# Retention queries and keys as a seven-product unit, T4 of the projections summed by DMA, and the norm2 transposes inside w_o

## The chip, the cores and the metric

The kernel runs on one core of one Trainium2 chip. The metric is the device time of one execution in microseconds, median of three runs. In the text TensorE is PE (its weight loads PEld), VectorE is DVE, ScalarE is ACT, GpSimd is POOL and SyncE is SP. DMAs are issued from SP's queue, and those that add to what lies in SBUF from POOL's.

## The reference, cut to what matters

One decoder block on x of 512 tokens by 1024 features, all in float32:

```python
h = rmsnorm(x, norm1_w)
rq, rk, rv, rg, mq, mk, mv, ga, gb = split(h @ w_in)   # 512, 512, 1024, 1024, 512, 512, 512, 1024, 1024 columns
rq = rotary(rq); rk = rotary(rk) * 128**-0.5            # 4 heads of 128
a = (silu(rg) * groupnorm(retention(rq, rk, rv))) @ w_ret_out
b = moba_attention(rmsnorm(mq), rmsnorm(mk), mv) @ w_moba_out   # 8 heads of 64, causal
x = x + (sigmoid(ga) * a + sigmoid(gb) * b) @ w_o
h2 = rmsnorm(x, norm2_w)
x = x + (silu(h2 @ w_ffn_gate) * (h2 @ w_ffn_up)) @ w_ffn_down  # hidden size 2816

def rotary(x):           # per head; halves of the 128 features
    return concat([x1 * cos - x2 * sin, x2 * cos + x1 * sin])
```

## The kernel before

**Products.** Every float32 operand is split in a high part of reduced precision and a rest, and a product of two tiles is three matmuls (high by high, high by rest, rest by high). A matrix product is cut in quarters, two by two. A plain quarter product takes eight block products. Most products use the Winograd variant of Strassen's method instead, with seven, named B11, T1, T2, B21, B22, T3 and T4 after the weight quarter or the sum of weight quarters that each uses; `wino_unit` issues them in the order of a string such as `NORMAL = "B11 T1 *1 T2 B21 B22 T3 / T4"`. What stands behind the slash, T4, is put off: it is issued at the `*1` of the next unit. Seven products of 24 matmuls of 256 columns make a unit, 168 matmuls.

**Weights.** A tile `raw` of 128 by 1024 comes by DMA. Its high part `wh` is a cast on ACT, its rest `wl` is a subtraction on DVE, and PE reads both. The sums T1 and T3 of two quarters come ready from the DMA: SP loads one quarter and POOL's DMA adds the other. T2 is T1 plus B22, and T4 is T2 plus B21, each an addition on DVE over 1024 columns (`make_sum`). In some units of the feed-forward part T4 is made by a third DMA on POOL instead, once T2 has been split (`t4dma`, `was_split`).

**Stages.** First come the queries and keys of MoBA, 47 us in (weights moving, plain product). Then follow projection units of 512 columns by a table, `ORDER`: rg 0, rk 0, rv 0, gb 0, rk 1, rv 1, rg 1, gb 1, then the output products b, ga, a. All are seven-product units except rk 0 and rk 1 (retention queries and keys of two heads each) and the output products a and b, which are plain: `feat_blocks` takes 32 weight tiles one by one, and each meets both token halves, six matmuls of 256 columns, 192 in a unit. Then w_o (`ALONE` order, 512 columns wide, 24 matmuls a product), the norm2 transposes, and the feed-forward part in four chunks, of which the last ends in an `ALONE` unit as well.

**Order.** Each engine runs its instructions in the order in which the code issues them. `advance` is called after each group of matmuls: it steps the weight pieces, with at most `AHEAD = (3, 4)` split pieces ahead of PE, and fires what `later(n, ...)` put off by n steps. `run_bg(1)` takes one step of background work (attention, retention scores and values, gates): after every 12 matmuls in a seven-product unit, after every 24 in a plain one.

**Around the change.** `rot_out` applies the rotary form to a finished group. In `wino_unit` the first product of a unit is copied into the bank Z by ACT (`p1`), and B21 accumulates on it. In `ALONE` units the last product, T4w, goes to banks W of its own, and DVE adds the shared part from X to the output tile beforehand (`u3`). `h2_turn(0)` transposes the upper token half after w_o's last product, with PE, four times four 128-column transposes; ACT makes the high parts `h` from them, DVE the rests, and the first feed-forward unit (`plain_unit`) needs both.

Of the kernel before, what the change touches and what calls it, by code (L numbers as in the profile page):

```python
# [42 lines left out]
ORDER = (("rg", 0), ("rk", 0), ("rv", 0), ("gb", 0), ("rk", 1), ("rv", 1), ("rg", 1), ("gb", 1), ("b", 0), ("b", 1), ("ga", 0), ("a", 0), ("ga", 1), ("a", 1))  # L43
WRQ = (0, 0)
RLAG = (1, 2, 3)
# [32 lines left out]
DOWN = "B11 B21 T1 T2 B22 T3 / T4"  # L78
ALONE = "B11 B21 T1 T2 B22 T3 T4w"


def weight_plan():
# [31 lines left out]
    for name, i in ORDER:  # L114
        if name == "rg":
            cols(C_RG + 512 * i)
        elif name == "rv":
            cols(C_RV + 512 * i)
        elif name == "rk" and WRQ[i]:
            wino("w_in", C_RQ + 256 * i, "w_in", C_RK + 256 * i)  # L120
        elif name == "rk":
            feat(sum([group("w_in", c + (2 * i + h) * P, KT) for h in (0, 1) for c in (C_RQ, C_RK)], []))
        elif name == "a":
            feat(sum([group("w_ret_out", (4 * i + ct) * P, KT) for ct in range(4)], []))
        elif name == "b":
# [41 lines left out]
def hybrid_block(ctx: ExitStack, tc: tile.TileContext, wall, xin, xtok, n2, cin, out):  # L167
# [108 lines left out]
    for u, unit in enumerate(plan):  # L276
        chunk_of[u] = chunk
        if unit[0] in "WX":
            ws = quarter_parts(unit)
            order = unit[2].split()  # L280
            if len(ws) > 1 or unit[2] == DOWN:
                t4dma.add(u)
# [13 lines left out]
            for q in order:  # L296
                if q == "/":
                    rest = True
                elif q[0] == "*":
                    for _ in range(int(q[1:])):  # L300
                        porder += left.pop(0) if left else []
                else:
                    x = [(u, (q[:3].rstrip("w"), j)) for j in range(len(ws))]
# [13 lines left out]
    assert not left  # L317
    wstate = {"next": 0, "live": 0, "cap": AHEAD, "load": 0, "drop": 0}
    wwait = []
# [400 lines left out]
    def feat_blocks(blocks, nbg=1):  # L720
# [3 lines left out]
        for b in blocks:  # L724
# [7 lines left out]
            mv = moving()  # L732
            if isinstance(mv, list):
                for i, m in enumerate(mv):
                    mm3(banks[g][:, i * 256:(i + 1) * 256], blk(u, pos % 16), m, first and i == 0, last, True)
            else:
                mm3(banks[g], blk(u, pos % 16), mv, first, last)
            pos += 1
# [52 lines left out]
    def wino_unit(w, ev, hooks={}):  # L791
# [13 lines left out]
        def third(*x):  # L805
            ev.c22(*x)
            if "T4w" in order:
                ev.u3(*x)

        def first(*x):  # L810
            ev.p1(*([*x, bank("Z")] if seed else x))

        whole = "T4w" in order
        seed = not wide and order[1] != "B21"
# [332 lines left out]
    def rot_out(h0):  # L1147
        def f(r, c, x):

            a, b = halves(nm("rot"))  # L1150
            hf = RDK // 2
            if h0 is None:
                c, h = c
                V.tensor_tensor(a, x, cosT, ALU.mult)
                V.tensor_tensor(b[:hf], x[hf:], sinT[hf:], ALU.mult)
                V.tensor_tensor(b[hf:], x[:hf], sinT[:hf], ALU.mult)
                V.tensor_tensor(a, a, b, ALU.add)
                (rqT, rkT)[c][h] = split(f"r{c}_{h}", a, None, SLAG[1])
                return
# [151 lines left out]

    def hmov(k):
        m = ("A11", "A21") if k < 4 else ("A12", "A22")
        return [hW(x, k % 4) for x in m]

    def rk_unit(n):
        h = 2 * n
        if WRQ[n]:
            wino_unit(hW, Quarters(rot_out(h)))
        else:  # L1320
            blocks = [((c, x), lambda k=k: hmov(k), k == 0, k == KT - 1,
                       lambda ps, c=c, x=x: later(1, lambda: rot_out(None)(0, (c, x), ps)))
                      for x in (h, h + 1) for c in (0, 1) for k in range(KT)]
            feat_blocks(blocks[:KT] + [wino_finish] + blocks[KT:])

# [102 lines left out]
    class Residual:  # L1428
# [29 lines left out]

        def u3(self, x, i):
            self.add(1, 0, x, i, ALU.add)  # L1460

        def c21w(self, w, i):
            self.add(1, 0, w, i, ALU.add, True)

        c21 = c21w

# [41 lines left out]
    def h2_turn(r):  # L1508

        pss, lows = [], []  # L1510
# [6 lines left out]
        for j in range(4):  # L1517
# [143 lines left out]
    for c in range(len(CHUNKS)):  # L1661
# [23 lines left out]
def _consts():  # L1685
# [60 lines left out]
```

## Time and profile before

| what | value |
|---|---|
| time, median of 3 runs | 794.83 us (792.03 to 795.05) |
| the profiled execution's own time | 794.83 us |
| its span, first to last instruction | 792.8 us |
| PE busy | 783.8 us, 99% |
| DVE busy | 648.2 us, 82% |
| ACT busy | 441.5 us, 56% |
| POOL busy | 64.9 us, 8% |
| DMA traffic | 126.47 MB, mean 160 GB/s |

The span is one execution. Outside it lie 2.0 us of that execution's time. A row's mean duration is from an instruction's start to its end; matmuls overlap, so that what a matmul costs PE is the distance from one start to the next. The busy share of PE counts a matmul's whole duration and says little on the rate; the idle time before an instruction, and what ended it, says where PE waited.

### The profile page before, as it was taken

How to read it: one execution, taken by the hardware profiler on the slowest of the kernel's cores; microseconds unless marked ns; L12 is line 12 of the kernel's file. 1: busy time of each engine (PE TensorE's matmuls, PEld its weight loads, DVE VectorE, ACT ScalarE, POOL GpSimd, SP SyncE). 2: the span in 40 equal slices, each digit the busy share in tenths (PEclk: the TensorE clock that was granted, in tenths of full speed). 3: DMA queues.
4: the chain of work that ended last, by engine and by line, in shares of the span. 5: the costliest groups of instructions: out<-in, count | busy, mean ns of one | idle time of the engine just before them, and what ended most of it. 6: DMA issues, size and time to landing. Idle time of an engine off the chain costs nothing.

```text
span 792.8 us, 13679 instructions
## 1 busy us (share of the span) xinstructions
PE 783.8 (99%) x5410; PEld 722.4 (91%) x5410; DVE 648.2 (82%) x978; ACT 441.5 (56%) x722; POOL 64.9 (8%) x85
## 2 busy tenths in 40 slices
PE   9999999999999999999999899999999999999998
PEld 6889998889999998998988799988999899988996
DVE  7889877977788678867679979889887988879787
ACT  8556764757437458643445566535554455644551
POOL 0004000000000000000001000011101110111000
PEclk9999999999999999999999999999999999999999
DMA  9843451524526546372899903589846893679602
GB/s 324 247 118 69 133 120 42 132 64 146 138 74 166 134 148 145 112 182 76 243 335 242 247 1 81 148 212 279 225 107 172 212 309 101 165 196 289 139 1 106
DMA packets 38223, 126.47 MB, mean 160 GB/s; under 512 B 4240, under 2 KB 4496, under 8 KB 38160
## 3 DMA queue, kind: packets, MB, share of 16 engines
q1 hardware_dynamic: 28224, 92.83, 33.8%
q0 software_dynamic: 9360, 31.72, 23.1%
q10 hardware_dynamic: 576, 1.05, 0.4%
q8 instruction: 42, 0.69, 0.4%
q14 instruction: 21, 0.17, 0.1%
HBM read 123.49 MB, written 2.10 MB: 158 GB/s over the span
## 4 chain that ended last, share of the span: by engine, by line
PE 91%; DVE 5%; DMA 2%; ACT 1%; issue 1%; SPq 0%; ACTq 0%
PE pm L219 82%; PE ps L219 8%; DMA raw<-wall 2%; DVE wl L219 1%; DVE h L219 1%; DMA xv<-xin 1%; DVE ws L219 1%; DVE xr L219 0%; DVE raw L219 0%; ACT sqh L911 0%; ACT wh L408 0%; ACT h L1503 0%; DVE xn L219 0%; DVE fb L219 0%; DVE gs L219 0%
## 5 line engine op out<-in xcount | busy, mean ns | idle before, releaser
L219 DVE TENSOR_TENSOR wl<-raw,wh 128x1024 fp32r<-128x1024 f32 x203 | 245.8, 1221 | 39.1 <-ACT wh L408 32.9
L408 ACT CAST wh<-raw 128x1024 fp32r<-128x1024 f32 (+1 forms) x224 | 219.3, 1006 | 62.4 <-DVE raw L219 38.3
L219 PE MATMUL pm<-h,wh 128*128 128x256 f32 x1248 | 226.9, 284 | 2.8 <-DVE h L219 1.5
L219 PEld LDWEIGHTS pm<-h,wh 128*128 128x128 f32 x1248 | 196.3, 193 | 3.9 <-DVE h L219 1.7
L219 PE MATMUL pm<-h,wl 128*128 128x256 f32 x624 | 177.2, 284 | 0.0
L219 PEld LDWEIGHTS pm<-h,wl 128*128 128x128 f32 x624 | 120.5, 193 | 0.0
L335 POOL DMA_DIRECT2D raw<-wall x56 | 49.3, 881 | 596.7 <-DMA raw<-wall 289.1
L219 PE MATMUL pm<-hA,wh 128*128 128x256 f32 x448 | 83.1, 285 | 0.0
L219 PEld LDWEIGHTS pm<-hA,wh 128*128 128x128 f32 x448 | 70.2, 191 | 1.1 <-issue 0.5
L219 PE MATMUL pm<-wh,hA 128*128 128x256 f32 (+1 forms) x304 | 69.3, 310 | 0.0
L219 PE MATMUL pm<-hA,wl 128*128 128x256 f32 x224 | 63.4, 283 | 0.0
L219 PE MATMUL pm<-wh,hS 128*128 128x256 f32 x320 | 62.8, 287 | 0.4 <-ACT pm L867 0.4
L219 DVE TENSOR_TENSOR raw<-raw,raw 128x1024 f32<-128x1024 f32 (+1 forms) x47 | 55.7, 1188 | 0.8
L219 PEld LDWEIGHTS pm<-wh,hA 128*128 128x128 f32 x304 | 51.1, 191 | 2.5
L219 PEld LDWEIGHTS pm<-wh,hS 128*128 128x128 f32 x320 | 51.6, 191 | 0.8 <-ACT pm L867 0.6
L219 DVE TENSOR_TENSOR xr<-xr,pm 128x512 f32<-128x512 f32 x74 | 48.2, 682 | 1.2 <-PE pm L219 1.0
L219 PE MATMUL pm<-hS,wh 128*128 128x256 f32 x256 | 47.3, 285 | 0.0
L219 PE MATMUL pm<-wl,hA 128*128 128x256 f32 (+1 forms) x152 | 46.5, 306 | 0.0
L219 PE MATMUL pm<-wl,hS 128*128 128x256 f32 x160 | 45.3, 283 | 0.3 <-DVE wl L219 0.3
L219 PEld LDWEIGHTS pm<-hA,wl 128*128 128x128 f32 x224 | 42.8, 191 | 0.0
L219 PEld LDWEIGHTS pm<-hS,wh 128*128 128x128 f32 x256 | 40.0, 192 | 0.1
L219 PE MATMUL pm<-wh,gsh 128*128 128x512 f32 x112 | 39.9, 391 | 0.0
(266 smaller groups left out, 1399.9 us busy)
## 6 DMA issues: line engine op xcount, KB each, us to landing
raw<-wall SPq DMA_DIRECT2D x153, 512.0 KB, 4.8
raw<-wall POOLq DMA_DIRECT2D x56, 512.0 KB, 7.2
raw<-wall SPq DMA_DIRECT2D x19, 256.0 KB, 4.0
raw<-wall POOLq DMA_DIRECT2D x9, 256.0 KB, 6.6
xr<-xtok SPq DMA_DIRECT2D x4, 512.0 KB, 7.2
out<-xr SPq DMA_DIRECT2D x8, 256.0 KB, 2.2
x<-xin SPq DMA_DIRECT2D x7, 256.0 KB, 4.8
raw<-wall ACTq DMA_DIRECT2D x4, 256.0 KB, 6.2
```

Source lines behind the costliest of these rows:

```text
L219: return f(out, *args, **kw)
L335: nc.gpsimd.dma_start(t[:, s], wall[c, :, s], accum_op=ALU.add)
L408: A.copy(h, src)
```

## The change

- Both rk units become seven-product units (`WRQ` and the plain branch are gone). `rot_out` works on one quarter at a time. The two halves of the 128 features are swapped by two ACT copies, and DVE multiplies the swapped tile by a sine table whose signs are exchanged.
- T4 of the projection units up to the first `ga` (`chunk < T4CHUNKS`) is made by a DMA on POOL, not by DVE.
- While MoBA's queries and keys are computed, five to six split pieces may be ahead (`EARLY`), and the extra `raw` tile is requested one product earlier.
- In `ALONE` units T4 (now `T4z`) accumulates in Z: ACT copies the shared part from X to Z, and `u3` on DVE is gone.
- The upper half's transposes come in four steps, the first of them in w_o's last product, the others behind it; then follow four matmuls of 512 columns on zeros (`FILL`), into the bank that the feed-forward part takes next.

```diff
+EARLY = (5, 6)
-WRQ = (0, 0)
+T4CHUNKS = 52
+FILL = 4
-ALONE = "B11 B21 T1 T2 B22 T3 T4w"
+ALONE = "B11 B21 T1 T2 B22 T3 T4z"
...
-        elif name == "rk" and WRQ[i]:
+        elif name == "rk":
             wino("w_in", C_RQ + 256 * i, "w_in", C_RK + 256 * i)
-        elif name == "rk":
-            feat(sum([group("w_in", c + (2 * i + h) * P, KT) for h in (0, 1) for c in (C_RQ, C_RK)], []))
...
-            if len(ws) > 1 or unit[2] == DOWN:
+            if len(ws) > 1 or unit[2] == DOWN or chunk < T4CHUNKS:
                 t4dma.add(u)
...
-    wstate = {"next": 0, "live": 0, "cap": AHEAD, "load": 0, "drop": 0}
+    wstate = {"next": 0, "live": 0, "cap": EARLY, "load": 0, "drop": 0}
...
             ev.c22(*x)
             if "T4w" in order:
                 ev.u3(*x)
+            elif "T4z" in order:
+                banks_, i = x
+                A.copy(bank("Z")[i], banks_[i])
...
-                 "T4w": ("W", "A22", True, True, getattr(ev, "c21w", None))}
+                 "T4w": ("W", "A22", True, True, getattr(ev, "c21w", None)),
+                 "T4z": ("Z", "A22", False, True, ev.c21)}
...
     tok_double(lambda k: mw[k], qk_evac(0, qraw))
+    more_raws(EXTRA)
...
-    more_raws(EXTRA)
+    wstate["cap"] = AHEAD
     mv_ev = Quarters(mv_out)
...
             cos, sin = (y[:, r * 256:(r + 1) * 256].unsqueeze(1).to_broadcast([P, 2, 256]) for y in (cosT, sinT))
+            A.copy(b[:hf], x[hf:])
+            A.copy(b[hf:], x[:hf])
             V.tensor_tensor(two(a), two(x), cos, ALU.mult)
-            V.tensor_tensor(two(b)[:hf], two(x)[hf:], sin[hf:], ALU.mult)
-            V.tensor_tensor(two(b)[hf:], two(x)[:hf], sin[:hf], ALU.mult)
+            V.tensor_tensor(two(b), two(b), sin, ALU.mult)
             V.tensor_tensor(a, a, b, ALU.add)
...
     def rk_unit(n):
...
+        wino_unit(hW, Quarters(rot_out(2 * n)))
...
+        def step(j):
             pss.append(turned(r, j))
             h2_put(("A11", "A12", "A21", "A22")[2 * r + j // 2], j % 2, pss[j])()
             if j:
                 keep(j - 1)
...
+        return [lambda j=j: step(j) for j in range(4)]
...
-    wino_unit(mx, Residual(squares))
-    for _ in range(100):
-        if complete.count(0) < 4:
-            later_step()
-    assert complete.count(0) == 4
-    h2_turn(0)
+    turn = h2_turn(0)
...
+    wino_unit(mx, Residual(squares), {"T3": lambda: bg.extend([None, None, turn_step])})
+    while turn:
+        turn_step()
+    spare = main_ps()
+    for _ in range(FILL):
+        nc.tensor.matmul(spare, lhsT=warmb[:, :P], rhs=warmb, start=True, stop=True)
```

What the change moves is seen at three places. The first is DVE at the seam from rk 1 to rv 1. `wl_2727` and `wl_2824` before are the rests of rv 1's T1 and T2; `rot`, `r` are a rotary group and its rest, `dia` and `sc` are retention scores. Before:

```order
L219 TENSOR_TENSOR wl_2727<-raw_2414,wh_2684 128x1024
L219 TENSOR_TENSOR sc_2690<-dia_2691,sc_2690 128x128
L219 SCALAR_TENSOR_TENSOR dia_2733<-ps_2729,sk,cst 128x128
L219 TENSOR_TENSOR raw_2414<-raw_2414,raw_2458 128x1024
L219 TENSOR_TENSOR r_2_2734<-rot_2706,r_2_2734 128x512
L219 TENSOR_TENSOR sc_2653<-dia_2733,sc_2653 128x128
L219 TENSOR_TENSOR rot_2779<-pm_2692,cs 128x512
L219 TENSOR_TENSOR rot_2779<-pm_2692,cs 64x512 x2
L219 TENSOR_TENSOR rot_2779<-rot_2779 128x512
L219 TENSOR_TENSOR wl_2824<-raw_2414,wh_2796 128x1024
```

After, the rest of rv 1's T2 is `wl_2927`; `pm_2471` in the first row is the bank of rk 1's T3, `qa_850` and `qb_851` are gates of the first two heads:

```order
L219 TENSOR_TENSOR qb_2470<-qa_2469,pm_2471 128x512
L219 SCALAR_TENSOR_TENSOR qa_850<-qa_850,r_y,sg_2840 128x256 x2
L219 TENSOR_TENSOR rL_2_2839<-rot_2832,rH_2_2838 128x2x256
L219 TENSOR_TENSOR rot_2878<-qb_2470,cs 128x512
L219 TENSOR_TENSOR rot_2878<-rot_2878,cs 128x512
L219 TENSOR_TENSOR rot_2878<-rot_2878 128x512
L219 SCALAR_TENSOR_TENSOR qa_850<-qa_850,r_y,sg_2862 128x256 x2
L219 TENSOR_TENSOR raw_2595<-raw_2595,raw_2647 128x1024
L219 SCALAR_TENSOR_TENSOR qb_851<-qb_851,r_y,sg_2887 128x256 x2
L219 TENSOR_TENSOR rL_2_2839<-rot_2878,rH_2_2838 128x2x256
L219 SCALAR_TENSOR_TENSOR qb_851<-qb_851,r_y,sg_2909 128x256 x2
L219 TENSOR_TENSOR wl_2927<-raw_2595,wh_2907 128x1024
```

The rotary groups of rk 1 now read what T3 leaves, the gates of the first two heads stand among them, and all of it stands ahead of the rest of rv 1's T2.

The second place is ACT in w_o's T3 and T4. `sq` are squares of the output rows, `r_s` the root of the upper half's norm, `wh` casts of feed-forward weights, `h` high parts of the transposed half. Before:

```order
L1472 ACTIVATE sq_5049,ss_4786<-xr_4777 128x512
L501 ACTIVATE r_s<-n2v 128x2
L408 CAST wh_5069<-raw_4797 128x1024
L408 CAST wh_5089<-raw_4812 128x1024
L408 CAST wh_5112<-raw_4896 128x1024
L1472 ACTIVATE sq_5120,ss_4786<-xr_4778 128x512
L1472 ACTIVATE sq_5132,ss_4786<-xr_4779 128x512
L408 CAST wh_5135<-raw_4920 128x1024
L1503 CAST h_640_5142<-ps_5137 128x512
```

After, where `pm_233` and `pm_4866` are the two banks Z:

```order
L1450 ACTIVATE sq_5055,ss_4792<-xr_4783 128x512
L501 ACTIVATE r_s<-n2v 128x2
L408 CAST wh_5075<-raw_4803 128x1024
L807 COPY pm_233<-pm_4806 128x512
L408 CAST wh_5095<-raw_4818 128x1024
L807 COPY pm_4866<-pm_4807 128x512
L408 CAST wh_5116<-raw_4902 128x1024
L1450 ACTIVATE sq_5124,ss_4792<-xr_4784 128x512
L1481 CAST h_650_5135<-ps_5130 128x512
L1450 ACTIVATE sq_5144,ss_4792<-xr_4785 128x512
L408 CAST wh_5147<-raw_4926 128x1024
L1481 CAST h_654_5154<-ps_5149 128x512
```

The two copies to Z, without which w_o's last product can't start, stand behind the norm's root and one and two weight casts; the first high part has one square and one cast fewer ahead of it.

The third place is PE at the end of w_o's last product, where `ps` rows are the transposes. Before (the eight transposes that follow are of the same kind):

```order
L219 MATMUL pm_5092<-wh_4989,mx_4867 128x512
L219 MATMUL pm_5092<-wl_4998,mx_4867 128x512
L219 MATMUL pm_5092<-wh_4989,mx_4867 128x512 x2
L219 MATMUL pm_5092<-wl_4998,mx_4867 128x512
L219 MATMUL pm_5092<-wh_4989,mx_4867 128x512
L219 MATMUL ps_5137<-cst,xn_5063 128x128
L219 MATMUL ps_5137<-cst,xn_5064 128x128
```

After (twelve transposes and the four matmuls on zeros follow):

```order
L219 MATMUL pm_233<-wh_4995,mx_4873 128x512
L219 MATMUL ps_5130<-cst,xn_5069 128x128
L219 MATMUL ps_5130<-cst,xn_5070 128x128
L219 MATMUL pm_4866<-wh_4995,mx_4873 128x512
L219 MATMUL pm_4866<-wl_5004,mx_4873 128x512
L219 MATMUL pm_4866<-wh_4995,mx_4873 128x512 x2
L219 MATMUL pm_4866<-wl_5004,mx_4873 128x512
L219 MATMUL pm_4866<-wh_4995,mx_4873 128x512
L219 MATMUL ps_5149<-cst,xn_5069 128x128
```

Four transposes moved ahead of the last six matmuls of the product; they were behind them.

## Rows read from the trace of the kernel before

**Rows 1.** The page, part 1: busy us (share) xinstructions.

```profile
PE 783.8 (99%) x5410; PEld 722.4 (91%) x5410; DVE 648.2 (82%) x978; ACT 441.5 (56%) x722; POOL 64.9 (8%) x85
```

**Rows 2.** Waits of PE by releaser: us in total, times, longest us.

```profile
PE pm L219 <- DVE h L219: 1.5, 1, 1.5
...
PE pm L219 <- ACT h L1503: 1.1, 1, 1.1
PE pm L219 <- ACT pm L867: 0.4, 1, 0.4
PE pm L219 <- DVE wl L219: 0.3, 1, 0.3
```

**Rows 3.** Timeline of PE in rk 1: start, us, instruction [idle before].

```profile
216.35 0.40 PE L219 MATMUL pm<-hA,wh 128*128 128x256 f32 x2
216.59 0.28 PE L219 MATMUL pm<-hA,wl 128*128 128x256 f32 x1
216.71 0.40 PE L219 MATMUL pm<-hA,wh 128*128 128x256 f32 x2
```

**Rows 4.** Groups of DVE by form: busy, mean ns | idle before.

```profile
L219 DVE TENSOR_TENSOR wl<-raw,wh 128x1024 fp32r<-128x1024 f32 x203 | 245.8, 1221 | 39.1 <-ACT wh L408 32.9 <-PE pm L219 3.2 <-PE ps L219 1.2
L219 DVE TENSOR_TENSOR raw<-raw,raw 128x1024 f32<-128x1024 f32 x44 | 53.8, 1223 | 0.8
...
L219 DVE TENSOR_TENSOR rot<-pm,cs 64x512 f32<-64x512 f32 x16 | 11.0, 688 | 0.2
...
L219 DVE TENSOR_TENSOR qb<-qa,pm 128x512 f32<-128x512 f32 x9 | 6.2, 683 | 0.8 <-PE pm L219 0.8
...
L219 DVE TENSOR_TENSOR r<-rot,r 128x512 fp32r<-128x512 f32 x8 | 5.4, 680 | 1.9 <-ACT r L479 1.9
...
L219 DVE SCALAR_TENSOR_TENSOR qa<-qa,r_y,sg 128x256 f32<-128x256 f32 x8 | 3.5, 482 | 0.1
```

**Rows 5.** Groups of ACT by form.

```profile
L408 ACT CAST wh<-raw 128x1024 fp32r<-128x1024 f32 x203 | 208.2, 1046 | 55.7 <-DVE raw L219 36.4 <-DMA raw<-wall 9.1 <-PE pm L219 4.6
...
L867 ACT COPY pm<-pm 128x512 f32<-128x512 f32 x9 | 5.3, 587 | 0.3 <-PE pm L219 0.3
```

**Rows 6.** Timeline, all engines, 450.3 to 455.5 us.

```profile
449.90 1.87 DVE L219 TENSOR_TENSOR xr<-xr,pm 128x512 f32<-128x512 f32 x3
...
450.35 1.91 PE L219 MATMUL ps<-cst,xn 128*128 128x128 f32 x16
...
452.77 1.06 ACT L1503 CAST h<-ps 128x512 fp32r<-128x512 f32 x2
...
453.40 0.38 PE L219 MATMUL pm<-h,wh 128*128 128x256 f32 x1 [1.14 <-ACT h L1503]
...
454.56 1.28 DVE L219 TENSOR_TENSOR h<-ps,h 128x512 fp32r<-128x512 f32 x2
...
455.30 0.39 PE L219 MATMUL pm<-h,wh 128*128 128x256 f32 x1 [1.51 <-DVE h L219]
```

**Rows 7.** Windows: us, busy of the five engines (x), PEclk, DMA, GB/s.

```profile
456.00:460.00 4.00, 4.00 (x23) 4.00 (x22) 3.18 (x5) 3.63 (x9) 0.00 (x0) 0.57 0.00 0
```

**Rows 8.** Timeline, all engines, 444.2 to 445.3 us.

```profile
444.28 0.20 ACT L501 ACTIVATE r_s<-n2v 128x2 f32<-128x2 f32 x1 [0.63 <-DVE n2v L219]
444.39 1.04 ACT L408 CAST wh<-raw 128x1024 fp32r<-128x1024 f32 x1
444.45 0.39 PE L219 MATMUL pm<-wl,mx 128*128 128x512 f32 x1
...
445.13 0.39 PE L219 MATMUL pm<-wl,mx 128*128 128x512 f32 x1
```

**Rows 9.** DMA issues: KB each, median us to landing.

```profile
raw<-wall SPq DMA_DIRECT2D x153, 512.0 KB, 4.8
raw<-wall POOLq DMA_DIRECT2D x56, 512.0 KB, 7.2
```

**Rows 10.** POOL by line: busy, mean ns | idle before, releasers.

```profile
L335 POOL DMA_DIRECT2D raw<-wall x56 | 49.3, 881 | 596.7 <-DMA raw<-wall 289.1 <-DVE wl L219 71.3 <-PE pm L219 47.0
```

More of the change, by code (lines that the diff above doesn't have):

```diff
@@ L302, in hybrid_block @@
                 else:
-                    x = [(u, (q[:3].rstrip("w"), j)) for j in range(len(ws))]
+                    x = [(u, (q[:3].rstrip("wz"), j)) for j in range(len(ws))]
                     if rest:
@@ L732, in feat_blocks @@
             mv = moving()
[L733 to L737, printed above, removed]
+            mm3(banks[g], blk(u, pos % 16), mv, first, last)
             pos += 1
@@ L808, in third @@
                 ev.u3(*x)
+            elif "T4z" in order:
+                banks_, i = x
+                A.copy(bank("Z")[i], banks_[i])
         def first(*x):
             ev.p1(*([*x, bank("Z")] if seed else x))
-        whole = "T4w" in order
+        whole = "T4w" in order or "T4z" in order
         seed = not wide and order[1] != "B21"
@@ L818, in wino_unit @@
                  "T4": ("X", "A22", False, True, ev.c21),
-                 "T4w": ("W", "A22", True, True, getattr(ev, "c21w", None))}
+                 "T4w": ("W", "A22", True, True, getattr(ev, "c21w", None)),
+                 "T4z": ("Z", "A22", False, True, ev.c21)}
         def run(q):
             b, m, start, stop, out = table[q]
-            wino_prod(w, u, bank(b), m, q.rstrip("w"), start, stop, out)
+            wino_prod(w, u, bank(b), m, q.rstrip("wz"), start, stop, out)
         rest = False
@@ L837, in wino_unit, with plain_unit @@
                     hooks[q]()
-    def plain_unit(w, ev, before_last):
+    def plain_unit(w, ev, before_last, pss):
         u = cur[0]
@@ L844, in plain_unit @@
             for n, out in enumerate((ev.gate, ev.up)):
-                ps = main_ps()
+                ps = pss.pop() if pss else main_ps()
                 for x, q in enumerate((("B11", "B21"), ("B12", "B22"))[n]):
@@ L1310, in ret_finish @@
                 bg.append(lambda f=n - RNORM: ret_transpose(f))
-    def hmov(k):
-        m = ("A11", "A21") if k < 4 else ("A12", "A22")
-        return [hW(x, k % 4) for x in m]
     def rk_unit(n):
[L1317 to L1324, printed above, removed]
+        wino_unit(hW, Quarters(rot_out(2 * n)))
     def rv_unit(n):
@@ L1457, in c22, with c21 @@
             self.add(1, 1, x, i, ALU.subtract, True)
[L1459 to L1465, printed above, removed]
+        def c21(self, x, i):
+            self.add(1, 0, x, i, ALU.add, True)
     ss2 = cp.tile([P, NT, 2], F32, name="ss2")
@@ L1508, in h2_turn @@
     def h2_turn(r):
-        pss, lows = [], []
+        pss = []
         def keep(j):
@@ L1515, in keep @@
             A.copy(f2[r, j], pss[j])
-        for j in range(4):
+        def step(j):
             pss.append(turned(r, j))
@@ L1521, in h2_turn @@
                 keep(j - 1)
-        keep(3)
-        del xn[2 * r], xn[2 * r + 1]
+            if j == 3:
+                keep(3)
+                del xn[2 * r], xn[2 * r + 1]
+        return [lambda j=j: step(j) for j in range(4)]
     def h2_lower():
-        h2_turn(1)
+        for f in h2_turn(1):
+            f()
         s, lows = {}, []
@@ L1553, in hybrid_block, with turn_step @@
     A.activation(warm, warm, AF.Sqrt)
-    wino_unit(mx, Residual(squares))
-    for _ in range(100):
-        if complete.count(0) < 4:
-            later_step()
-    assert complete.count(0) == 4
-    h2_turn(0)
+    turn = h2_turn(0)
+    def turn_step():
+        for _ in range(100):
+            if complete.count(0) < 4:
+                later_step()
+        assert complete.count(0) == 4
+        turn.pop(0)()
+    wino_unit(mx, Residual(squares), {"T3": lambda: bg.extend([None, None, turn_step])})
[4 more added lines that the diff above has]
+        nc.tensor.matmul(spare, lhsT=warmb[:, :P], rhs=warmb, start=True, stop=True)
     class Hidden:
@@ L1674, in hybrid_block @@
                 wstate["cap"] = PAHEAD
-                plain_unit(h2, Hidden(mats, k), h2_lower)
+                plain_unit(h2, Hidden(mats, k), h2_lower, [spare])
             else:
@@ L1692, in _consts @@
     c[:half, K_COS:K_COS + S] = c[half:, K_COS:K_COS + S] = np.cos(ang)
-    c[:half, K_SIN:K_SIN + S] = np.sin(ang)
-    c[half:, K_SIN:K_SIN + S] = -np.sin(ang)
+    c[:half, K_SIN:K_SIN + S] = -np.sin(ang)
+    c[half:, K_SIN:K_SIN + S] = np.sin(ang)
     c[:, K_TRI:K_TRI + P] = p[None, :] >= p[:, None]
```

8 lines of the change are left out of this document (removed).

## The prediction

> **What bounds the kernel now.** I read the busy times first. PE is busy for 783.8 of 792.8 us and the next engine, DVE, for 648.2 [rows 1], so the time is what PE has to do, plus the few places where it stands still. PE's rate comes from the distance of starts in a stretch without idle time: three matmuls of 256 columns from 216.35 to 216.71, so 0.12 us each [rows 3]. Then PE's waits: the four that the change can touch are 1.5 and 1.1 us for high parts and rests of the transposed norm2 half, 0.4 us for a copy of ACT and 0.3 us for one rest [rows 2]. The third view is the granted clock by windows: in the four microseconds behind the two longest of these waits it is 0.57, between the levels 1.2 and 2.4 GHz [rows 7]; at the full level the same matmuls would have ended 4.00 x (1 - 0.57) = 1.7 us sooner. So there are three ways to gain: fewer matmuls, less idle time, and no slow stretch behind it. And one way to lose: DVE, ACT or the weight queue become late where PE now does the same work in less time.
>
> The sum is made against the profiled execution, which is also the median: 794.83 us, of which 2.0 us lie outside its span.
>
> **Fewer matmuls.** Each rk unit falls from 192 to 168 matmuls of 256 columns. That is 48 x 0.12 = 5.76 us off PE [rows 3]. It holds only if everything that feeds PE keeps up; the next steps look at that.
>
> **The seam from rk 1 to rv 1.** As a plain unit, rk finished a group after each eight weight tiles, and the rotary work was spread over the unit. As a seven-product unit it leaves most of that work to its end: T3 completes banks at the end, and T4 is put off into the next unit. From T3's end PE has three products, rv 1's B11 and T1 and rk 1's T4, before rv 1's T2: 3 x 24 x 0.12 = 8.64 us. There is no attention left to stretch them here. T2 needs its rest, and ahead of that DVE has, from the order: one `qb` at 0.68, eight gate steps at 0.48, two rests of `r` at 0.68, three rotary steps at 0.69, a weight sum at 1.22 and the rest itself at 1.22 [rows 4]. That is 0.68 + 3.86 + 1.36 + 2.07 + 1.22 + 1.22 = 10.4 us against 8.64: 1.8 us too much by itself. DVE begins up to one weight rest (1.22) and one matmul's end (0.40, [rows 3]) late, and one ACT copy lies between the rotary steps, at 0.59 by the nearest copy [rows 5]: 10.4 + 1.6 + 0.6 - 8.64 = 4.0. Three sums back to back took 1.87 us, a spacing of 0.60 where one takes 0.68 [rows 6]; 16 instructions tighter by 0.09 give 1.4 back, 2.5 us. I take 2.7, near this last value. Lower bound 0, if gates and rotary steps find DVE idle within the unit; upper bound 5.6, if two copies and a cast of 1.05 [rows 5] stand in a row with it. What is queued behind the late rest on DVE is the weight work of rv 1, and PE is the one that waits.
>
> At the seam from rk 0 to rv 0 the same DVE work stands, but attention matmuls lie between the products and lengthen PE's side. I take 0, with an upper bound of 1.5, about half the other seam.
>
> The rotary edit itself takes 16 half-tile DVE steps away and puts ACT copies of about 0.59 in their place. ACT is busy for 56% [rows 1], so the copies cost nothing but the latency that is counted above; without that cover each unit's eight would be 8 x 0.59 = 4.7 us, and they would show as ACT's copies ahead of weight casts.
>
> **T4 by DMA, and the early pieces.** The eight T4 sums taken from DVE are worth 8 x 1.22 us there [rows 4], and two T2 sums and six more rests come back with the rk units, so DVE gains almost nothing: (-8 + 2 + 6) x 1.22 = 0. What it adds is ten DMAs in POOL's queue, with an issue of 0.88 each [rows 10], and four for rk's T1 and T3. I count it at 0: the sum behind the slash is used a unit later, and a landing of 7.2 us [rows 9] has that long. If that cover is gone it is the last rival below. The earlier pieces can take away the two early waits, 0.4 and 0.3 us [rows 2], which come just when pieces are made as fast as they are used. Bounds 0 and 0.7; I take 0.4.
>
> **The end of w_o.** Before, T4 ends at 450.35, the 16 transposes take 1.91, PE waits 1.14 and 1.51, and steady work begins at 455.30 [rows 6]. With the clock's 1.7 and less the 0.12 already done that is worth a start at 456.9. After, T4 accumulates in Z and can't begin before ACT has copied X there. The copy stands behind the norm's root at 444.28 and a weight cast that starts at 444.39 and takes 1.04 [rows 8]: 445.43 + 0.59 = 446.0, where PE comes for it at 444.9, since T3's matmuls of 512 columns run 0.227 us apart, three from 444.45 to 445.13. So PE waits 1.2 us there, and 0.2 more after six matmuls, because the second copy is behind one more cast. Then 24 x 0.227 = 5.44, the transposes 1.91 as before and four matmuls on zeros 4 x 0.227 = 0.91: 446.1 + 0.2 + 5.44 + 1.91 + 0.91 = 454.6. Gain 456.9 - 454.6 = 2.3 us. By then the first high parts have been made during the last product, and the square and cast that stood ahead of them are behind. Bounds: 0.6 if the clock still falls (1.7 back), 3.7 if the copies don't wait.
>
> The trace has PE idle for 2.65 us (453.40 and 455.30, [rows 6]) and then a clock of 0.57 [rows 7]. The Trainium skill says (TensorE: Matmul & The Clock Gate, Part 1: The HAM clock gate) that the array's default is the lower of two clocks and that activity releases it. The row agrees; by that rule the stall at rv 1 would add the slow stretch's 1.7 us, 790.8 in all.
>
> **Sum.** 794.83 - 5.76 - 0.4 + 2.7 - 2.3 = 789.1 us.
>
> **Rivals.**
> *All is hidden.* DVE does the gates and rotary steps in gaps and PE never waits at rv 1: 794.83 - 5.76 - 0.4 - 2.3 = 786.4, and 785.0 if the Z copies don't wait either. For it: DVE sits idle 39.1 us ahead of rests [rows 4], so it has room somewhere. Against: the order puts the 10.4 us just here.
>
> *Both seams jam and the clock falls.* PE waits 1.5 at rv 0, 2.7 at rv 1, and pays one slow stretch of 1.7: 794.83 - 5.76 - 0.4 + 1.5 + 4.4 - 2.3 = 792.3. The fewer matmuls are then mostly a new wait. For it: the slow stretch [rows 7] shows that a wait of this size has cost such a stretch. Against: attention covers rv 0.
>
> *POOL's queue becomes the bound (slower).* A unit's T1 and T3 need SP's load and POOL's add, 4.8 + 7.2 = 12.0 us [rows 9], and if POOL must first issue T4's DMA, which waits for T2's split, 0.88 more [rows 10]. Four products last 4 x 2.88 = 11.5 us. Where the queue has no lead, T3's sum is 12.0 + 0.9 - 11.5 = 1.4 us late in every unit; in the six units without attention 8.4 us: 789.1 + 8.4 = 797.5, slower than before. It decides once POOL is held by T4's wait while the next T1's load has landed. For it: POOL's idle time ahead of its issues is mostly waits for loads and rests, in order. Against: loads come several tiles ahead, and POOL is busy for 8%.
>
> The Trainium skill (SBUF — State Buffer, SBUF: two separate sides) states that DMAs issued from GpSimd can't have their descriptors written while VectorE runs an operation that takes the shared port pair. Landing from POOL takes 7.2 where SP's take 4.8 [rows 9], which fits but doesn't prove it; by that rule ten more DMAs would fall in a stretch where DVE is busy, and the last rival would be likelier.
>
> **How the numbers follow.** The forecast (787 to 791, 789.1 as its centre) gets 0.45; all hidden 0.22; both seams jam 0.22; POOL's queue 0.11. The range 784.5 to 794.5 holds the first and most of the next two, and leaves out the POOL case and thin ends, 0.18 in all. A difference of 0.5%, 4.0 us, is about what a measurement can tell from no change; so faster is below 790.9 and slower above 798.8. Faster: 0.42 of the forecast, 0.22 hidden, 0.02 of the jam, 0.66. Slower: half of the POOL case with a later queue than worked out, 0.06. Same: 0.28.
>
> **What would show it.** PE's matmul count falls by 44, and rk's stretches run at 0.12. PE's waits show one for `wl` in rv 1's T2 of 2 to 4 us; if it is under 1, the seam was wrong. Ahead of w_o's last product PE waits for ACT's copy for about 1.2 us; the waits for `h` are gone and the clock behind w_o is near 1. If the clock is still low there, the gain of 2.3 was too high. A wait of PE for `raw` or its cast in rg 1, gb 1 or ga 0 would speak for POOL's queue. The prediction is wrong as a whole if the time leaves 784.5 to 794.5, or if the clock is low in a stretch that isn't named here.

## The result and the profile after

The changed kernel takes 805.83 us, the kernel before 794.0 us beside it: a ratio of 1.0144 (95% interval 1.0119 to 1.0170), so the change makes it 1.4% slower. The forecast was 789.1 us with a range of 784.5 to 794.5.

PE's part of the page answers to [rows 1]. The 44 matmuls are gone, and still the span grew from 792.8 to 804.1 us:

```profile
span 804.1 us, 13646 instructions
PE 783.6 (97%) x5366; PEld 720.5 (90%) x5366; DVE 642.8 (80%) x970; ACT 461.4 (57%) x754; POOL 77.5 (10%) x99
```

The waits of PE (releaser: us in total, times, longest us) answer to [rows 2]. The four that the change could touch are gone, and six others of 0.8 us or more stand in their place (what the lines leave out lies in the first 8 us or is 0.3 us or less):

```profile
PE pm L219 <- ACT pm L807: 5.7, 1, 5.7
PE pm L219 <- DVE wl L219: 2.1, 1, 2.1
PE ps L219 <- ACT p L1043: 2.0, 1, 2.0
PE ps L219 <- ACT pt L1080: 1.7, 1, 1.7
PE pm L219 <- ACT wh L408: 1.2, 1, 1.2
...
PE ps L219 <- DVE moT L219: 0.8, 1, 0.8
```

They lie in three places, and at each the clock is low. The windows have the columns of [rows 7] (us, busy of PE, PEld, DVE, ACT, POOL, then the granted clock):

```profile
140.00:152.00 12.00, 7.20 (x53) 6.32 (x53) 11.13 (x23) 7.74 (x20) 0.00 (x0) 0.97 0.18 49
152.00:156.00 4.00, 4.00 (x22) 3.38 (x22) 3.16 (x7) 3.33 (x10) 1.76 (x2) 0.67 0.71 174
...
240.00:244.00 4.00, 2.80 (x13) 2.80 (x14) 3.20 (x5) 3.02 (x5) 1.76 (x2) 0.50 0.19 24
244.00:248.00 4.00, 4.00 (x25) 4.00 (x25) 3.94 (x5) 2.86 (x4) 0.00 (x0) 0.64 0.94 219
...
456.00:460.00 4.00, 2.82 (x7) 2.24 (x8) 2.77 (x4) 3.44 (x6) 0.86 (x1) 0.50 0.58 125
460.00:464.00 4.00, 4.00 (x18) 3.22 (x16) 0.80 (x1) 0.17 (x2) 0.00 (x0) 0.77 0.49 93
```

In the kernel before, PE never waits in the first two of these stretches:

```profile
140.00:152.00 12.00, 12.00 (x87) 9.72 (x85) 11.22 (x22) 8.14 (x21) 0.86 (x1) 1.00 0.42 105
240.00:244.00 4.00, 4.00 (x36) 4.00 (x35) 3.41 (x7) 3.87 (x9) 0.01 (x1) 1.00 0.56 175
```

Where the time went is read from the distance of the two traces: how much later the same matmul starts in the changed kernel. A row gives what the distance grows by in that place. At the seams from rk 0 to rv 0 ("end of rk 0") and from rk 1 to rv 1 ("rv 1's T2") background work has moved as well, so these two rows are the waits and the clock's loss instead, which is a window's length times one minus its granted clock:

| place | distance, us | what it consists of |
|---|---|---|
| up to 67 us | -1.2 | the two early waits are gone |
| both rk units | -5.8 | 48 matmuls of 0.12 |
| end of rk 0 | +6.5 | waits of 0.3 + 0.8 + 2.0 + 1.7, and 12 x 0.03 + 4 x 0.33 of clock |
| rv 1's T2 | +6.0 | waits of 1.2 + 2.1, the rest clock |
| end of w_o | +4.4 | a wait of 5.7, low clock behind it, less what the new end gives |

These sum to +9.9 of the 11.3 us in span; 1.4 is not assigned. At w_o's first matmul the distance is 6.4 us (412.24 us before, 418.65 after) and in the feed-forward part 10.8.

**The end of w_o.** The timeline of ACT (start, us, instruction, idle before):

```profile
450.82 0.20 ACT L501 ACTIVATE r_s<-n2v 128x2 f32<-128x2 f32 x1 [0.62 <-DVE n2v L219]
450.93 1.03 ACT L408 CAST wh<-raw 128x1024 fp32r<-128x1024 f32 x1
456.56 0.57 ACT L807 COPY pm<-pm 128x512 f32<-128x512 f32 x1 [4.60 <-DVE xr L219]
```

DVE in the same stretch:

```profile
452.05 2.74 DVE L219 SCALAR_TENSOR_TENSOR xn<-xr,r_y,n2r 128x512 f32<-128x512 f32 x4
454.71 1.22 DVE L219 TENSOR_TENSOR wl<-raw,wh 128x1024 fp32r<-128x1024 f32 x1
455.84 1.28 DVE L219 TENSOR_TENSOR xr<-xr,pm 128x512 f32<-128x512 f32 x2
```

And PE:

```profile
457.18 0.79 PE L219 MATMUL pm<-wh,mx 128*128 128x512 f32 x1 [5.72 <-ACT pm L807]
...
467.41 0.59 PE L219 MATMUL pm<-h,wh 128*128 128x256 f32 x2
```

The copy from X to Z stands where it was expected on ACT, behind the root and one cast. But it then idles 4.60 us for DVE, which has to subtract the same bank X from the output rows first, and comes to that behind the four scaled rows and a rest. The last row shows the good side: the feed-forward part starts at 467.41 without the waits of [rows 6].

**rv 1's T2.** DVE has no idle time there but one short wait for ACT's swap, and all eight gate steps (`qa`, `qb`) lie in the stretch:

```profile
231.36 0.68 DVE L219 TENSOR_TENSOR qb<-qa,pm 128x512 f32<-128x512 f32 x1
231.96 0.88 DVE L219 SCALAR_TENSOR_TENSOR qa<-qa,r_y,sg 128x256 f32<-128x256 f32 x2
...
234.26 0.69 DVE L219 TENSOR_TENSOR rot<-rot,cs 128x512 f32<-128x512 f32 x1 [0.22 <-ACT rot L1155]
...
236.39 1.22 DVE L219 TENSOR_TENSOR raw<-raw,raw 128x1024 f32<-128x1024 f32 x1
...
239.93 2.36 DVE L219 TENSOR_TENSOR wl<-raw,wh 128x1024 fp32r<-128x1024 f32 x2
```

ACT stands idle for T2's sum, which ends at 237.6, before it can cast it; PE waits first for that cast, then for T2's rest:

```profile
237.64 1.04 ACT L408 CAST wh<-raw 128x1024 fp32r<-128x1024 f32 x1 [0.82 <-DVE raw L219]
238.74 0.39 PE L219 MATMUL pm<-wh,hS 128*128 128x256 f32 x1 [1.22 <-ACT wh L408]
241.20 0.58 PE L219 MATMUL pm<-wl,hS 128*128 128x256 f32 x1 [2.08 <-DVE wl L219]
```

**The end of rk 0.** DVE and ACT there, with PE's longest wait behind them:

```profile
144.29 0.69 DVE L219 TENSOR_TENSOR rot<-qb,cs 128x512 f32<-128x512 f32 x1
...
146.25 1.22 DVE L219 TENSOR_TENSOR raw<-raw,raw 128x1024 f32<-128x1024 f32 x1
147.39 0.68 DVE L219 TENSOR_REDUCE mx<-ps 128x1 f32<-128x512 f32 x1
...
148.36 0.78 ACT L1043 ACTIVATE p<-ps,nb,qs 128x512 f32<-128x512 f32 x1 [3.48 <-DVE rl L219]
...
149.28 0.66 PE L219 MATMUL ps<-cst,p 128*128 128x128 f32 x4 [1.98 <-ACT p L1043]
```

Three rotary steps and T2's weight sum, 3.1 us, stand ahead of the maximum of one softmax; ACT's exponentials wait for it, and PE, whose next work is the transposes of their result, waits for ACT. Rotary steps stand ahead of a maximum in the kernel before too, and PE doesn't wait there:

```profile
138.85 2.09 DVE L219 TENSOR_TENSOR rot<-pm,cs 128x512 f32<-128x512 f32 x3
...
141.58 0.68 DVE L219 TENSOR_REDUCE mx<-ps 128x2 f32<-128x512 f32 x1
```

The difference is how late DVE is by then: this maximum starts 3.0 us after PE has ended its scores (at 138.6 us), the one in the changed kernel 7.2 us after (at 140.2 us).

### The profile page after: what moved, and what is told of

Read it like the earlier page. It is cut to its first block, busy times and chain, and to the rows that moved or that the text cites. A ratio compares the mean times of both kernels' runs of the same rounds, so it can differ in the third digit from the quotient of the medians.

```text
span 804.1 us, 13646 instructions
## 1 busy us (share of the span) xinstructions
PE 783.6 (97%) x5366; PEld 720.5 (90%) x5366; DVE 642.8 (80%) x970; ACT 461.4 (57%) x754; POOL 77.5 (10%) x99
## 4 chain that ended last, share of the span: by engine, by line
PE 88%; DVE 7%; ACT 2%; issue 1%; DMA 1%; ACTq 0%; DVEq 0%
PE pm L219 81%; PE ps L219 7%; DVE wl L219 1%; DVE rot L219 1%; DVE h L219 1%; DMA xv<-xin 1%; DVE ws L219 1%; ACT wh L408 1%; DVE raw L219 0%; DVE qb L219 0%; DVE xr L219 0%; ACT p L1043 0%; DVE mx L219 0%; DVE xn L219 0%; DVE rL L219 0%
## 5 line engine op out<-in xcount | busy, mean ns | idle before, releaser
L219 DVE TENSOR_TENSOR wl<-raw,wh 128x1024 fp32r<-128x1024 f32 x209 | 252.5, 1221 | 42.9 <-ACT wh L408 35.8
L335 POOL DMA_DIRECT2D raw<-wall x60 | 55.7, 928 | 451.4 <-DMA raw<-wall 266.2
L219 PE MATMUL pm<-hS,wh 128*128 128x256 f32 x384 | 71.2, 286 | 0.0
L219 PEld LDWEIGHTS pm<-hS,wh 128*128 128x128 f32 x384 | 60.0, 191 | 0.6 <-issue 0.3
L219 PE MATMUL pm<-hA,wh 128*128 128x256 f32 x288 | 54.4, 288 | 0.0
L219 PE MATMUL pm<-hS,wl 128*128 128x256 f32 x192 | 54.3, 283 | 0.0
L219 DVE TENSOR_TENSOR raw<-raw,raw 128x1024 f32<-128x1024 f32 (+1 forms) x41 | 48.2, 1182 | 0.4
L219 PEld LDWEIGHTS pm<-hA,wh 128*128 128x128 f32 x288 | 45.8, 194 | 0.4
L219 PE MATMUL pm<-wh,mx 128*128 128x512 f32 x112 | 36.8, 407 | 5.7 <-ACT pm L807 5.7
L219 PE MATMUL pm<-hA,wl 128*128 128x256 f32 x144 | 41.0, 284 | 0.0
```

The lines of the kernel that those rows point to most:

```text
L219: return f(out, *args, **kw)
L335: nc.gpsimd.dma_start(t[:, s], wall[c, :, s], accum_op=ALU.add)
```

## The experiments

The kernel before ran beside each; its medians there were 793.3 to 795.0 us. The ratios are to it. Each run is the changed kernel with one or more edits: the runs named zf have the edit of z_first, and zf_gates, those named zfg and the two named rk0 have that of gates_late as well.

| kernel | us | ratio (95% interval) |
|---|---|---|
| changed kernel | 805.8 | 1.0144 (1.0119 to 1.0170) |
| z_first | 798.1 | 1.0043 (1.0026 to 1.0060) |
| gates_late | 801.3 | 1.0078 (1.0059 to 1.0096) |
| rk_plain | 802.1 | 1.0082 (1.0065 to 1.0099) |
| wo_old | 801.5 | 1.0071 (1.0048 to 1.0094) |
| zf_gates | 793.5 | 0.9999 (0.9987 to 1.0010) |
| zf_rot_dve | 798.7 | 1.0060 (1.0036 to 1.0083) |
| zf_slow_bg | 798.4 | 1.0053 (1.0034 to 1.0072) |
| zf_t4_dve | 799.8 | 1.0073 (1.0053 to 1.0092) |
| zfg_spread | 792.8 | 0.9980 (0.9968 to 0.9992) |
| zfg_nofill | 793.8 | 0.9986 (0.9975 to 0.9997) |
| rk0_dve | 788.5 | 0.9924 (0.9908 to 0.9940) |
| rk0_no_early | 789.2 | 0.9935 (0.9921 to 0.9949) |

**z_first: the copy ahead of the subtraction.**

```diff
         def third(*x):
+            if "T4z" in order:
+                banks_, i = x
+                A.copy(bank("Z")[i], banks_[i])
             ev.c22(*x)
             if "T4w" in order:
                 ev.u3(*x)
-            elif "T4z" in order:
-                banks_, i = x
-                A.copy(bank("Z")[i], banks_[i])
```

Expected:

> The changed kernel with one edit: in w_o's T3 the ACT copy from X to Z is issued ahead of DVE's subtraction of the same bank X. Theory: in the changed kernel the copy waits for that subtraction (ACT idle 4.60 us, ended by DVE's xr), which stands in DVE's queue behind the norm's root, four scaled rows and a weight rest. Issued first, the copy waits only for PE and for the casts ahead of it on ACT, so PE's wait of 5.72 us falls to 1 to 1.5 us, the clock stays up in the product (about 2.8 us), and the time is 805.8 - 4.3 - 2.8 = 798 to 800. Rival: the wait is one for the former content of Z or for the casts, not for the subtraction: PE's wait stays near 5.7 and the time near 805.8.

798.1 us, as the theory had it. The copy follows the cast at once, and the clock stays up in the product; ACT's row, and then the window:

```profile
450.85 0.58 ACT L804 COPY pm<-pm 128x512 f32<-128x512 f32 x1
```

```profile
452.00:456.00 4.00, 4.00 (x19) 3.07 (x19) 4.00 (x6) 2.35 (x4) 0.00 (x0) 1.00 1.07 294
```

In this trace PE has no wait above 0.1 us at that place; in those of the kernels built on it the wait is 0.4 to 1.1 us. The order of two reads of one bank, on two engines, was worth 7.7 us by the medians, 8.0 by the ratios. The Trainium skill (PSUM — Partial Sum Buffer, PSUM bank collisions raise a hardware error) says that two engines may not touch the same bank at once, reads included, so that such accesses are put in an order. The trace agrees that the copy waited for a read (4.60 us); that an overlap would be an error no run here shows.

**wo_old: the end of w_o as before.** T4w with `u3`, all transposes behind, no `FILL`.

```diff
-ALONE = "B11 B21 T1 T2 B22 T3 T4z"
+ALONE = "B11 B21 T1 T2 B22 T3 T4w"
...
-    wino_unit(mx, Residual(squares), {"T3": lambda: bg.extend([None, None, turn_step])})
+    wino_unit(mx, Residual(squares))
...
```

Expected:

> The changed kernel with the end of w_o as before: T4 in banks of its own, DVE adds the shared part beforehand, all transposes behind the product, no matmuls on zeros. Theory: the new end costs more than it gives: against before the changed kernel is 6.3 us behind at w_o's T3 and 11.0 us behind in the feed-forward part, so undoing it gives 805.8 - 4.7 = 801.1, with the waits of 1.1 and 1.5 us for the transposed half back. Rival: the low clock at T4 comes from the work ahead of it, not from the wait: then less than 2 us come back.

801.5 us, as expected: undone, the new end gives 4.3 us back (5.8 by the ratios), and the waits of 1.1 and 1.5 us of [rows 6] return. Against z_first it is 3.4 us slower by the medians and 2.2 by the ratios, but its runs lie between 798.6 and 802.6 us and the intervals overlap. The traces tell it better: from w_o's first matmul to the feed-forward part the distance to the kernel before stays at 6.8 us in wo_old, and falls from 6.6 to 3.0 in z_first. So the new end gives 3.5 us when the copy doesn't wait, near the 3.7 that the prediction had as its bound for that. In the traces where PE waits 0.4 to 1.1 us for the copy it gives 2.3 to 3.3; 2.3 were forecast.

**gates_late: the gates behind the seam.**

```diff
-RGATE = (2, 0)
+RGATE = (20, 0)
```

Expected:

> The changed kernel with one number changed: the gates of retention heads 0 and 1 are put off by 20 background steps instead of 2, so that their eight DVE steps and eight sigmoids on ACT stand behind the seam from rk 1 to rv 1. Theory: DVE's queue at that seam is too long by itself, 1.22 + 2.08 us of PE wait and some 2.8 us of low clock behind it. Eight gate steps are 8 x 0.44 = 3.5 us of DVE, so the waits fall under 0.5 us and the clock stays up: 805.8 - 6 = 799.5 to 801. Rival: the seam waits for weights (T4's DMA in POOL's queue, or the weight sum itself): waits of 3 us stay, time 804 to 807.

801.3 us, just above the 799.5 to 801 expected. Of the 3.3 us of waits at rv 1 one of 0.8 is left (at 239.2 us) where under 0.5 was expected, and the clock stays up:

```profile
PE pm L219 <- DVE wl L219: 0.8, 1, 0.8
```

```profile
240.00:244.00 4.00, 4.00 (x36) 4.00 (x35) 2.74 (x5) 1.88 (x4) 1.18 (x2) 1.00 0.74 143
```

**zf_gates: both edits.**

```diff
-RGATE = (2, 0)
+RGATE = (20, 0)
...
+            if "T4z" in order:
+                banks_, i = x
+                A.copy(bank("Z")[i], banks_[i])
             ev.c22(*x)
...
```

Expected:

> Two edits of the changed kernel together: the copy to Z ahead of DVE's subtraction, and the gates of heads 0 and 1 put off by 20 background steps. Theory: the two places don't touch each other, so the gains add: 798.1 - 4.5 = 793.6 us, with the waits in 140 to 152 us (4.8 us and some 3 us of low clock) as what is left of the loss. Rival: the gates put off displace other work and the end of w_o or rg 1 loses what rv 1 gains: 796 or more.

793.5 us: the two add. What remains of the loss are mostly the waits in 140 to 152 us and the low clock behind them; 0.8 us of wait stay at rv 1 and 1.0 at the copy.

**rk_plain: both rk units plain, the swap still on ACT.**

```diff
+RKP = (0, 1)
...
+        elif name == "rk" and i not in RKP:
+            wino("w_in", C_RQ + 256 * i, "w_in", C_RK + 256 * i)
         elif name == "rk":
-            wino("w_in", C_RQ + 256 * i, "w_in", C_RK + 256 * i)
+            feat(sum([group("w_in", c + (2 * i + h) * P, KT) for h in (0, 1) for c in (C_RQ, C_RK)], []))
...
```

Expected:

> The changed kernel with both rk units plain again, 192 matmuls each; the swap of the rotary halves by ACT, T4 by DMA, the early pieces and the new end of w_o stay. Theory: the waits at the end of rk 0 (4.8 us in 140 to 152 us, and about 1.5 us of low clock) and at rv 1 (3.3 us and 2.8 us of clock) come from what the seven-product units do to DVE, ACT and the attention steps, and go; 48 x 0.12 = 5.76 us of matmuls come back: 805.8 - 12.4 + 5.8 = 799. Rival: T4's DMAs in POOL's queue cause the waits: they stay in part and the time is 805 or more.

802.1 us, where 799 were expected. The waits at rv 1 are gone, but at the end of rk 0 3.2 us stay, which is the difference; the clock stays up there:

```profile
PE ps L222 <- ACT pt L1087: 1.6, 2, 1.4
PE ps L222 <- ACT p L1050: 1.6, 1, 1.6
```

In ACT's rows the two rotary copies stand ahead of the `pt` copies, and PE waits 1.4 us for these, until 142.5 us:

```profile
140.57 0.58 ACT L1162 COPY rot<-pm 64x512 f32<-64x512 f32 x1
141.16 0.58 ACT L1163 COPY rot<-pm 64x512 f32<-64x512 f32 x1
141.77 0.37 ACT L1082 COPY pt<-ps 128x256 f32<-128x256 f32 x1
```

So either the swap on ACT or another part of the change holds attention there, even in a plain unit; rk0_dve tells the two apart.

**zf_rot_dve: the swap on DVE again, in seven-product units.**

```diff
-            A.copy(b[:hf], x[hf:])
-            A.copy(b[hf:], x[:hf])
             V.tensor_tensor(two(a), two(x), cos, ALU.mult)
-            V.tensor_tensor(two(b), two(b), sin, ALU.mult)
+            V.tensor_tensor(two(b)[:hf], two(x)[hf:], sin[hf:], ALU.mult)
+            V.tensor_tensor(two(b)[hf:], two(x)[:hf], sin[:hf], ALU.mult)
...
```

Expected:

> The changed kernel with the copy to Z ahead of the subtraction, and the rotary halves swapped by DVE as before (two half-tile products, no ACT copies). It asks which part of the waits in 140 to 152 us comes from the swap on ACT. Theory: DVE stands still in its rotary steps until ACT has made the two copies (1.56 us idle at 137.5), and ACT makes them behind softmax steps; the softmax steps behind these on DVE then come late for PE. Without the copies the waits of PE there fall from 4.8 to under 2 us and the clock stays up: 798.1 - 5 = 793 us. Rival: the attention steps come every 12 matmuls instead of every 24 in a seven-product unit, and that alone makes PE wait for softmax: the waits stay at 4 us or more, time 797 to 799.

798.7 us: my theory, that the copies alone make the waits, fell. At the end of rk 0 4.8 us of waits stay, as in z_first (0.3, 2.8 and 1.7), and at rv 1 they grow from 3.3 to 4.6:

```profile
PE ps L219 <- ACT p L1043: 2.8, 1, 2.8
PE pm L219 <- ACT wh L408: 2.5, 1, 2.5
PE pm L219 <- DVE wl L219: 2.0, 1, 2.0
```

**zf_slow_bg: attention at the pace of the plain unit in rk 0** (`slow[0]` is set for that unit).

```diff
-                run_bg(1)
+                if not (slow[0] and i == 0):
+                    run_bg(1)
```

Expected:

> The changed kernel with the copy to Z ahead of the subtraction, and in rk 0 one background step per 24 matmuls instead of one per 12, as in the plain unit. Theory of the swap on ACT: waits stay at 2 us or more, since the copies still stand between the softmax steps; time 795 to 798. Theory of the pace of attention: the waits in 140 to 152 us go, with them the low clock: 798.1 - 4.8 - 3.4 = 790 us.

798.4 us: the pace of attention, the rival of the run before, doesn't make the waits alone either. With the copies still on ACT, waits of 4.3 us stay in 132 to 145 us, without a low clock, and at rv 1 they grow from 3.3 to 6.4 us, the longest 3.4 us for a rest at 247.8 us:

```profile
PE pm L219 <- DVE wl L219: 4.4, 2, 3.4
PE ps L219 <- ACT pt L1082: 1.7, 3, 1.1
PE pm L219 <- DVE moT L219: 1.6, 1, 1.6
```

**zfg_spread: rotary steps put off into rv 0.** zf_gates with

```diff
-            later(1, lambda: self.out(0, 1, b))
+            later(self.lag[0], lambda: self.out(0, 1, b))
...
-            later(1, lambda: self.out(1, 1, b))
+            later(self.lag[1], lambda: self.out(1, 1, b))
...
-        wino_unit(hW, Quarters(rot_out(2 * n)))
+        wino_unit(hW, Quarters(rot_out(2 * n), (5, 9) if n in (0, 1) else (1, 1)))
```

Expected:

> The copy to Z ahead of the subtraction, the gates put off by 20 steps, and in both rk units the rotary steps of the two quarters that lie in SBUF by then put off, from 1 to 5 and to 9 groups of 12 matmuls. Nothing else moves. Theory of bunching: DVE's work at the end of rk 0 is spread into rv 0, so softmax comes in time there and the waits of 4.8 us and 3.4 us of low clock fall by half or more: 787 to 790 us. Rival: the pace of attention in a seven-product unit keeps DVE and ACT full whatever the order: the waits move and stay as large, 792 to 795 us.

792.8 us, the rival's number: the waits move to 149 to 175 us and are larger, 6.2 us, the longest 3.2; no window there has a low clock, and that is what is saved.

**rk0_dve: only rk 0 as before.** zf_gates with rk 0 plain, as in rk_plain, and its swap on DVE (the sine table has the signs of the changed kernel, hence the subtraction):

```diff
+RKP = (0,)
...
+        elif name == "rk" and i not in RKP:
...
+            if h0 is None:
+                c, h = c
+                V.tensor_tensor(a, x, cosT, ALU.mult)
+                V.tensor_tensor(b[:hf], x[hf:], sinT[hf:], ALU.mult)
+                V.tensor_tensor(b[hf:], x[:hf], sinT[:hf], ALU.mult)
+                V.tensor_tensor(a, a, b, ALU.subtract)
...
```

Expected:

> The copy to Z ahead of the subtraction, the gates of heads 0 and 1 put off by 20 steps, and rk 0 alone a plain unit again with its rotary swap on DVE as before; rk 1 stays a seven-product unit with its swap on ACT. Theory: what is left of the loss lies at the end of rk 0, where the rotary steps of four quarters come together and stand between the softmax steps on DVE and ACT; with rk 0 as before, the waits of 4.8 us and the low clock of 3.4 us in 140 to 158 us go, and 24 x 0.12 = 2.9 us of matmuls come back: 793.5 - 8.2 + 2.9 = 788 us. Rival: the waits there come from T4's DMAs or from the early pieces that shift the stretch against attention: they stay, 796 us.

788.5 us, where 788 were expected, and faster than the kernel before by 0.76%. At the end of rk 0 one wait of 0.3 us is left:

```profile
PE ps L222 <- ACT pt L1082: 0.3, 1, 0.3
```

The early pieces and T4's DMAs are in it, except those of rk 0 itself, and zf_t4_dve below has the same waits with T4 on DVE; so neither makes them. In rk_plain, which at this place differs by the swap on ACT alone, the plain unit has 3.2 us of them. So each of the two edits by itself, the seven products (zf_rot_dve, 4.8 us) or the swap on ACT (rk_plain, 3.2), is enough to hold attention in rk 0, and only without both is it free. What it is in the seven products stays open: the pace of attention was slowed only with the copies on ACT in place (zf_slow_bg), and no run has the slow pace with the swap on DVE.

**zf_t4_dve: T4 of the projections on DVE.**

```diff
-T4CHUNKS = 52
+T4CHUNKS = 0
```

Expected:

> The changed kernel with the copy to Z ahead of the subtraction, and T4 of the projections added by DVE instead of by a DMA on POOL. Theory: POOL's queue costs PE nothing in the changed kernel, and the ten sums of 1.22 us go back to DVE, two of them at the seams that jam: 798 to 801 us, with a longer wait at rv 1. Rival (POOL's queue as the bound, from the prediction): waits for weights in rv 1 and behind it go, 793 to 796 us.

799.8 us, 1.7 above z_first; the intervals overlap, so the 1.7 is not shown by itself. The first wait at rv 1 grows from 1.2 to 2.1 us, and at the end of rk 0 the waits stay as they were. No wait goes away, as one would have to if POOL's queue made it; T4 by DMA helps at the seam.

```profile
PE pm L219 <- ACT wh L408: 2.1, 1, 2.1
...
PE ps L219 <- ACT p L1043: 2.0, 1, 2.0
```

**zfg_nofill: zf_gates without the matmuls on zeros.**

```diff
-FILL = 4
+FILL = 0
```

Expected:

> The copy to Z ahead of the subtraction, the gates put off by 20 steps, and no matmuls on zeros behind the transposes. Theory: the four matmuls cover a wait for the transposed half's first parts; without them PE waits some 0.9 us instead, the time stays at 793.5 within 0.5 us, unless the wait lowers the clock as before, which adds 1.7. Rival: the parts are ready anyway, and 0.9 us are gained: 792.6 us.

793.8 us, not to be told from zf_gates: 0.2 us slower by the medians, 1.0 faster by the ratios, with intervals that overlap. In place of the wait of 0.9 us that the theory had, one of 0.2 us stands at the first feed-forward matmuls, so the 0.9 us of work on zeros covers little.

**rk0_no_early: rk0_dve without the early pieces.**

```diff
-EARLY = (5, 6)
+EARLY = AHEAD
```

Expected:

> The best version so far (copy to Z ahead of the subtraction, gates put off by 20 steps, rk 0 plain with the swap on DVE; 788.5 us) without the early pieces: no more than three to four split pieces ahead from the start on, as before the change. Theory: the early pieces are what takes the two waits of 0.4 and 0.3 us behind 60 us away; without them these come back and the time is 788.9 to 789.7 us. Rival: T4 by DMA took them away, and the early pieces do nothing: 788.5 us and no such wait.

789.2 us, and one of the two early waits is back (0.4 us at 60.9). The direction fits; the intervals overlap, so the 0.7 us itself isn't shown.

## Why the prediction was wrong

- **Fewer matmuls, -5.76.** Right: both units show 168, at 0.12 us each.
- **The end of w_o, -2.3. This step failed.** The copy was priced by what stands ahead of it on ACT, 1.2 us. Its other wait was left out: DVE's subtraction of the same bank, issued one line earlier. DVE's queue at that place, the root chain, four scaled rows and a rest, was in the order, but was not read for this. Measured: a wait of 5.7 us and a low clock behind it, +4.4 in all, 6.7 us off the term. z_first shows the cause; with the copy first the new end gives 2.3 to 3.5 us.
- **The seam of rk 0, 0 with an upper bound of 1.5. This step failed as well.** The argument was that attention's matmuls lengthen PE's side and so cover DVE. They are no cover: they wait for softmax steps that stand in the same two queues, DVE's and ACT's, among the rotary work. Measured: waits of 4.8 us and a low clock, +6.5 in all. The runs show which edits do it, the seven products or the swap. How the seven products do it is open. The count over all units, (-8 + 2 + 6) x 1.22 = 0, hides that rk 0 gets 7 rests and a sum instead of 4 rests; but DVE is no busier in 140 to 152 us than before (11.13 us against 11.22), it is later.
- **The rotary copies, nothing but latency. Too cheap:** in a plain unit 3.2 us of waits stand with them (rk_plain) and 0.3 without (rk0_dve). In a seven-product unit taking them away gives nothing (zf_rot_dve).
- **The seam of rv 1, +2.7. The mechanism was right,** queue and all; the waits were 3.3 us. The term that was mis-sized is the clock, which the forecast left out and a rival held at 1.7: the seam cost 6.0.
- **Early waits, -0.4.** They went, and the distance was -1.2.
- **POOL's queue,** the slower rival at 797.5: it gave the direction, not the cause. zf_t4_dve is against it, and the landings from POOL took 7.4 us, hardly more than before.

The three terms that were off, by 6.7, 6.5 and 3.3 us, make 16.5 of the 16.7 us between forecast and result. The range was too narrow because the wait at w_o was bounded without DVE's queue, and because a slow stretch was allowed for at one place or the other, not at three. The rival in which both seams jam and the clock falls named what happened at the seams, but held it at 1.5, 2.7 and 1.7 us, 5.9 in all, where 12.5 were measured.

## What to carry to other kernels

When a copy or an accumulation makes an engine read a bank that another engine reads too, look which read is issued first, and price the wait by the other engine's queue, not by its own. Work on PE that depends on DVE and ACT was no cover here for more work on DVE and ACT. Where PE is the bound, a wait of a few microseconds is to be priced with a low clock behind it, but as a chance, not as a certainty.

## What the runs showed of the hardware

A wait doesn't always lower the clock. At waits of 2.0 and 1.7 us with four transposes between them, of 1.2 and 2.1 us, and of 5.7 us the granted clock fell in the changed kernel, to 0.67, 0.50 and 0.50 over four microseconds (0.50 is the lower level, 1.2 of 2.4 GHz). In rk_plain waits of 1.4 and 1.6 us within 5 us left it at 1.00, and in zfg_spread a single wait of 3.2 us did:

```profile
169.95 0.52 PE L219 MATMUL ps<-cst,p 128*128 128x128 f32 x3 [3.17 <-DVE p L219]
```

```profile
168.00:172.00 4.00, 2.05 (x18) 2.08 (x19) 3.86 (x9) 2.20 (x5) 0.24 (x1) 1.00 0.78 130
```

The Trainium skill (TensorE: Matmul & The Clock Gate, Part 1: The HAM clock gate) says that the clock is set by how busy PE has been recently. The three places in the changed kernel agree; why it stayed up in zfg_spread and rk_plain is open. Nor has the same wait always the same price: with the same two waits at the end of rk 0 (2.0 and 1.7 us) the window of 152 to 156 us has 0.67 in the changed kernel and 0.50 in zf_gates.

A copy of half a tile, 64 partitions by 512, took ACT 0.58 us out of the accumulator and 0.62 from SBUF, no less than the 0.59 of a whole one in [rows 5]: two half copies cost twice a whole one.
